# MLA layer: attention probabilities transposed by VectorE blocks and DMA instead of TensorE, with other DMA queues

## The chip, the cores and the metric

One core of one Trainium2 chip runs the whole program. The metric is the device time of one execution in microseconds (us); less is better.

## What is computed

The reference takes 512 tokens of width 1024 in fp32 through two layers and a last norm: an SSD (state space) layer, then a multi-head latent attention (MLA) layer with 16 heads. The change lies in the second layer:

```python
proj = u @ in_w
c_q, c_kv, k_r, z = proj[..., :o1], proj[..., o1:o2], proj[..., o2:o3], proj[..., o3:]
q = (rms_norm(c_q, q_norm_w) @ uq_w).reshape(bsz, seq, MLA_N_HEADS, MLA_QK_DIM)
kv = (rms_norm(c_kv, kv_norm_w) @ ukv_w).reshape(bsz, seq, MLA_N_HEADS, MLA_NOPE_DIM + MLA_V_DIM)
q_nope, q_rope = q[..., :MLA_NOPE_DIM], rope(q[..., MLA_NOPE_DIM:], positions)
o = causal_block_attention(q_full, k_full, v, MLA_QK_DIM ** -0.5)   # softmax in blocks of 128 queries
o = o.reshape(bsz, seq, MLA_WIDTH) * jax.nn.silu(z)
return o @ out_w
```

with 384 and 256 wide latents, head parts of 128 (plain) and 64 (rope), and values of 128.

## The kernel before

**Precision.** Every fp32 operand of a matmul is split into a high part in fp32r and the rest. ScalarE (ACT) casts the high part, VectorE (DVE) subtracts it to get the low part, and TensorE (PE) makes three passes: high by high, low by high, high by low. For weights this is `split_weight` (L266): a tile `raw` comes from HBM, ACT writes `whi` (L272), DVE writes `wlo` (L273). The pools hold 2 `raw`, 3 `whi` and 3 `wlo`; weights are loaded and split one ahead of their use (`LOOK`, `prefetch`). So the `whi` of a weight takes the buffer of the weight three before it, and can be written only when that one's gemm is done.

**Order.** PE's order is written by hand: it is the order in which the program issues its matmuls. DVE, ACT and the DMA queue of SyncE (SP) are ordered by a scheduler when the program is built; on the chip each engine takes its instructions strictly in that order. In the second layer everything that is in PSUM outside a few special tiles goes through `bank`, eight buffers of 128x512.

**A head.** The main loop (L884 and on) takes one head `h` at a time. Its gemms, the `feed`, belong to later heads: an even head runs `front_a` of the next pair of heads (the rope part `rraw`, the query `qh`/`ql`, the key `k`, with the weight `ua`) and a gemm for the gate `z`; an odd head runs `front_b` (query, key with the weight `ub`, and both halves of the values `va`/`vb` with the weight `uc`) and a gemm for `z`. Heads 11 to 15 have pieces of the output projection in place of gemms that have run out. Between the gemms `sched` (L237) places attention work: each piece stands at a fraction of the head's cost, from the tables at the top: `SC` for the four score blocks of the *next* head, `TU` for the four `turn` calls and `PR` for the four `product` calls of this head.

- `score(h, b)` makes scores of 128 queries by n keys on PE, a masked max on DVE (L805), the exp with its sum on ACT (L223), a reciprocal (L807) and a scale (L808) on DVE. The result `p` has queries in partitions.
- `turn(h, kb)` has PE transpose the blocks of key block `kb` (L817, ten 128x128 transposes a head) into a bank `pt`; ACT casts `ph` from it (L821), DVE subtracts `pl` (L822). `ph` and `pl` have two buffers each.
- `product(h, kb)` adds three matmuls to the head's bank `po` (L835): `ph` by `va`, `ph` by `vb`, `pl` by `va`. After the fourth, DVE multiplies `po` by `z` (L837).
- `rope` (L692) copies `rraw` with halves exchanged into `rsw`, by four DMAs, and makes two products and a sum on DVE (L697 to L699). `front_a` calls it once a pair of heads.

**Early in the layer** the first layer's output, transposed in 32x32 blocks by DVE into `ht` (L681), is stored by 32 small DMAs to `hd` in DRAM (L684): each writes 32 partitions of 16 blocks, which undoes the block order.

All of these DMAs, the weights included, go through SP's queue.

Of the kernel before, what the change touches and what calls it, by code (L numbers as in the profile page):

```python
# [10 lines left out]
F32 = mybir.dt.float32  # L11
F32R = mybir.dt.float32r
AF = mybir.ActivationFunctionType
ALU = mybir.AluOpType

P = 128
T = 512
D = 1024
KD = D // P
NCH = T // P  # L20
# [3 lines left out]
MH = 16  # L24
QL, KVL = 384, 256
# [14 lines left out]
P1 = (1.0, 2.4, 3.8, 12.0, 18.2)  # L40
GN = 16.84
G7 = 33.0
SF = (0.02, 0.1, 2.1, 3.1)
SC = (0.0, 0.16, 0.25, 0.44)
TU = (0.02, 0.08, 0.38, 0.55)
PR = (0.3, 0.48, 0.65, 0.94)
KO = (3, 4, 5, 8, 10)
MID = 4
NU = 1
# [2 lines left out]
SQ = 2  # L52
# [99 lines left out]
class Net:  # L152
# [8 lines left out]
    def build(self):  # L161
        tc, nc, ctx = self.tc, self.nc, self.ctx
        pool = lambda name, bufs, **k: ctx.enter_context(tc.tile_pool(name=name, bufs=bufs, **k))
        self.const = pool("const", 1)
        self.wraw = pool("wraw", 2)
        self.whi = pool("whi", 3)
        self.wlo = pool("wlo", 3)
        self.act = pool("act", 8)
        self.o16 = pool("o16", 16)
        self.nrm = pool("nrm", 1)  # L170
        self.res = pool("res", 8)
        self.dram = pool("dram", 1, space=bass.MemoryType.DRAM)

        const = self.const
        self.xs = []
        self.cols = const.tile([P, C_N], F32, name="cols")
        self.ident = const.tile([P, P], F32, name="ident")[:]
        self.rows = const.tile([P, 2 * NH], F32, name="rows")

        self.phase, self.group, self.before, self.head = "", [], [], None  # L180
        self.wq = []
        self.wpos = self.wload = 0
        self.wraws = []
        self.wready = {}
        for g in range(NG):
            for i in range(6):
                self.wq.append(("w", U_IN + 6 * g + i))
        for i in range(16):
            self.wq.append(("w", U_OUT0 + i))
        for i in range(6):  # L190
            self.wq.append(("w", U_M1 + i))
        self.wq += [("w", U_MZ + i) for i in range(3)] + [("ua", 0), ("w", U_MZ + 3), ("ub", 0), ("uc", 0), ("w", U_MZ + 4)]
        out = [("w", U_OUT1 + i) for i in range(16)]
        for h in range(14):
            j = h // 2 + 1
            self.wq += [("ua", j)] if h % 2 == 0 else [("ub", j), ("uc", j)]
            if h < 11:
                self.wq.append(("w", U_MZ + 5 + h))
            self.wq += [out.pop(0) for _ in range({11: 1, 12: 1, 13: 2}.get(h, 0))]
        self.wq += out  # L200

        with tc.tile_pool(name="ps_s", bufs=1, space=bass.MemoryType.PSUM) as ps, \
                tc.tile_pool(name="ssm", bufs=2) as wk:
            self.ps, self.wk = ps, wk
            self.ssm()
        with tc.tile_pool(name="ps_m", bufs=1, space=bass.MemoryType.PSUM, reuse_waits="tile") as ps, \
                tc.tile_pool(name="mla", bufs=2, reuse_waits="tile") as wk:
            self.ps, self.wk = ps, wk
            self.mla()

    LOOK = 1

# [47 lines left out]
    def load_weight(self, kind, idx):  # L260
        n = {"w": 1024, "ua": 1024, "ub": 640, "uc": 512}[kind]
        raw = self.wraw.tile([P, n], F32, tag="raw", name=self.nm("raw"))
        self.nc.sync.dma_start(raw[:], self.t[kind][idx])
        return raw

    def split_weight(self, raw, cuts=()):  # L266
# [383 lines left out]
    def mla(self):  # L650
        tc, nc, t, wk = self.tc, self.nc, self.t, self.wk
        v = nc.vector
        self.bufs = {"b": 8}
        col = lambda i: self.cols[:, i:i + 1]
        con = wk.tile([P, K_N - K_MASK], F32, name="con2", bufs=1)
        nc.sync.dma_start(con[:], t["con"][:, K_MASK:])
# [14 lines left out]
        for i in range(6):  # L671
            w = self.weight("w", U_M1 + i)
            ps = self.bank("mm")
            self.run(self.gemm(ps[:], w, vh, vl, KD))
            if i == NU:
                pss = self.sumsq([h[:] for h in self.h], D, "b")
                r1 = self.rstd_of(pss, D)
            if i >= 2:
                for k in (2 * i - 4, 2 * i - 3):
                    ht = wk.tile([P, T], F32, tag=("ph", "pl")[k % 2], name=self.nm("ht"))  # L680
                    v.transpose(ht[:], self.h[k][:])  # L681
                    for b in range(4):
                        m = slice(32 * b, 32 * b + 32)
                        nc.sync.dma_start(turned[:, :, k * P + 32 * b:k * P + 32 * b + 32],  # L684
                                          ht[m, :].rearrange("a (j b) -> a j b", b=32))
            pend.append(ps)
            while pend and i >= NU:
                o = self.o16.tile([P, T], F32, tag="o", name=self.nm("cq"))
                v.tensor_tensor(o[:], pend.pop(0)[:], r1[:], op=ALU.mult)
                cq.append(o)  # L690

        def rope(raw):  # L692
            sw = wk.tile([P, T], F32, tag="rsw", name=self.nm("rsw"), bufs=1)
            for i in range(4):
                j = i ^ 1
                nc.sync.dma_start(sw[32 * i:32 * i + 32, :], raw[32 * j:32 * j + 32, :])
            v.tensor_tensor(raw[:], raw[:], self.cosT, op=ALU.mult)  # L697
            v.tensor_tensor(sw[:], sw[:], self.sinT, op=ALU.mult)
            v.tensor_tensor(raw[:], raw[:], sw[:], op=ALU.add)  # L699
            return raw  # L700
# [77 lines left out]
                f["v"].append((va, vb))  # L778
                yield 1.3

        probs = [[] for _ in range(MH)]

        def score(h, b):
            f, i = F[h // 2], h % 2
# [21 lines left out]
            self.E(p[:], p[:], AF.Exp, scale=-1.0, bias=st[:, 0:1], accum_out=st[:, 1:2])  # L806
            v.reciprocal(st[:, 2:3], st[:, 1:2])  # L807
            v.tensor_scalar(p[:], p[:], st[:, 2:3], None, op0=ALU.mult)  # L808
            probs[h].append(p)

        parts, acc = [[] for _ in range(MH)], {}

        def turn(h, kb):
            n = T - kb * P
            pt = self.bank("pt")
            for b in range(kb, NCH):
                nc.tensor.transpose(pt[:, (b - kb) * P:(b - kb + 1) * P], probs[h][b][:, kb * P:(kb + 1) * P],  # L817
                                    self.ident)
            ph = wk.tile([P, T], F32R, tag="ph", name=self.nm("ph"))
            pl = wk.tile([P, T], F32R, tag="pl", name=self.nm("pl"))  # L820
            nc.scalar.copy(ph[:, :n], pt[:, :n])  # L821
            v.tensor_tensor(pl[:, :n], pt[:, :n], ph[:, :n].bitcast(F32), op=ALU.subtract)  # L822
            parts[h].append((ph, pl))

        def product(h, kb):
# [13 lines left out]
        def chain(*gs):  # L839
            for g in gs:  # L840
                yield from g
# [4 lines left out]
            yield from self.out_tok(zt, 0, hd)  # L846

        def norm(tiles, n, cw):
            at = (wk, ("qh", "ql", "s2") if n == KVL else ("ph", "pl", "s2"))
            pss = self.sumsq([x[:] for x in tiles], n, "b", *at)  # L850
            r = self.rstd_of(pss, n, *at)
            hs, ls = [], []
            for i, x in enumerate(tiles):
                v.scalar_tensor_tensor(x[:], x[:], col(cw + i), r[:], op0=ALU.mult, op1=ALU.mult)
                a = wk.tile([P, T], F32R, tag="ch", name=self.nm("ch"), bufs=5)
                b = wk.tile([P, T], F32R, tag="cl", name=self.nm("cl"), bufs=5)
                nc.scalar.copy(a[:], x[:])
                v.tensor_tensor(b[:], x[:], a[:].bitcast(F32), op=ALU.subtract)
                hs.append(a)
                ls.append(b)  # L860
            return hs, ls

        outg = out0()
        self.run(zgemm(0))
# [15 lines left out]
        self.run(zgemm(3))  # L880
        zsilu(0)
        self.run(fa)
        self.run(front_b(0))
        self.sched(zgemm(4), [(x, functools.partial(score, 0, b)) for b, x in enumerate(SF)])  # L884
        for h in range(MH):
            if h and h % 4 == 0:
                zsilu(h // 4)
            feed, cost = [], 0.0
            j = h // 2 + 1
            if h < 14:  # L890
                feed.append(front_a(j) if h % 2 == 0 else front_b(j))
                cost += 5.2 if h % 2 == 0 else 5.9
            if h < 11:
                feed.append(zgemm(5 + h))
                cost += 5.2
            if h >= 11:
                k = KO[h - 11]
                feed.append(itertools.islice(outg, k))
                cost += 1.3 * k
            at = SC if h + 1 < MH else ()  # L900
            pieces = [(x * cost, functools.partial(score, h + 1, b)) for b, x in enumerate(at)]
            pieces += [(x * cost, functools.partial(turn, h, b)) for b, x in enumerate(TU)]
            pieces += [(x * cost, functools.partial(product, h, b)) for b, x in enumerate(PR)]
            self.sched(chain(*feed), pieces)
# [166 lines left out]
```

## Time and profile before

| what | value |
|---|---|
| median of 3 runs | 837.02 us (836.73 to 837.34) |
| the profiled execution | 836.13 us |
| its span in the trace | 834.0 us |
| mean granted PE clock | 0.999 |
| PE busy | 819.3 us (98%) |
| DVE busy | 644.9 us (77%) |
| ACT busy | 450.4 us (54%) |
| GpSimd (POOL) busy | 0.2 us |
| DMA, share of 16 engines, queue of SP | 34.0% |

The profiled execution is one of many, and 2.1 us of its time lie outside the span. "Busy" of PE counts matmuls whose ends are modelled, so consecutive matmuls overlap in the records: a row's duration is longer than its place, which is the distance between two starts. Times in the timeline count from the start of the span. A group's row gives count, busy us and mean ns of one, and then the idle time of its engine just before it with what ended it. A name such as `ph<-pt` is output from input, by the program's tile names.

### The profile page before, as it was taken

How to read it: one execution, taken by the hardware profiler on the slowest of the kernel's cores; microseconds unless marked ns; L12 is line 12 of the kernel's file. 1: busy time of each engine (PE TensorE's matmuls, PEld its weight loads, DVE VectorE, ACT ScalarE, POOL GpSimd, SP SyncE). 2: the span in 40 equal slices, each digit the busy share in tenths (PEclk: the TensorE clock that was granted, in tenths of full speed). 3: DMA queues.
4: the chain of work that ended last, by engine and by line, in shares of the span. 5: the costliest groups of instructions: out<-in, count | busy, mean ns of one | idle time of the engine just before them, and what ended most of it. 6: DMA issues, size and time to landing. Idle time of an engine off the chain costs nothing.

```text
span 834.0 us, 11549 instructions
## 1 busy us (share of the span) xinstructions
PE 819.3 (98%) x4228; PEld 691.8 (83%) x4228; DVE 644.9 (77%) x1234; ACT 450.4 (54%) x794; POOL 0.2 (0%) x4
## 2 busy tenths in 40 slices
PE   7999999999999999999999999999999999999996
PEld 5887888888888888888888888888888888888885
DVE  7999898979787989778566787786767869675544
ACT  7567755545465657434353654556547557554233
POOL 0000000000000000000000000000000000000000
PEclk9999999999999999999999999999999999999999
DMA  6364543423242423333555142222222224331212
GB/s 227 103 191 141 155 147 106 152 99 129 101 139 90 152 76 127 115 121 94 130 130 132 54 130 64 79 72 76 63 64 58 90 78 152 101 97 56 86 66 101
DMA packets 50856, 90.55 MB, mean 109 GB/s; under 512 B 21552, under 2 KB 23088, under 8 KB 50800
## 3 DMA queue, kind: packets, MB, share of 16 engines
q1 hardware_dynamic: 50080, 88.77, 34.0%
q10 hardware_dynamic: 720, 1.05, 0.3%
q8 instruction: 33, 0.54, 0.3%
q14 instruction: 23, 0.19, 0.1%
HBM read 83.12 MB, written 4.33 MB: 105 GB/s over the span
## 4 chain that ended last, share of the span: by engine, by line
PE 92%; DVE 3%; DMA 2%; ACT 1%; SPq 1%; issue 0%; DVEq 0%; ACTq 0%
PE mm L291 55%; PE ot L941 11%; PE s L793 5%; PE mm L300 4%; PE po L835 4%; PE mm L773 3%; PE pt L817 2%; PE yd L138 2%; PE yd L291 1%; PE aux L130 1%; PE aux L105 1%; DMA x<-in_x_dram 1%; PE aux L77 1%; PE aux L89 1%; DMA L<-ac_d 1%; DVE wlo L273 1%
## 5 line engine op out<-in xcount | busy, mean ns | idle before, releaser
L272 ACT CAST whi<-raw 128x1024 fp32r<-128x1024 f32 (+3 forms) x132 | 127.0, 965 | 210.3 <-PE mm L291 172.8
L273 DVE TENSOR_TENSOR wlo<-raw,whi 128x1024 fp32r<-128x1024 f32 (+3 forms) x132 | 146.8, 1115 | 54.6 <-ACT whi L272 54.3
L291 PE MATMUL mm<-ah,whi 128*128 128x512 f32 x384 | 154.0, 401 | 0.0
L291 PE MATMUL mm<-ah,wlo 128*128 128x512 f32 x384 | 150.3, 391 | 0.4 <-DVE wlo L273 0.4
L291 PE MATMUL mm<-al,whi 128*128 128x512 f32 x384 | 149.9, 390 | 0.0
L291 PE MATMUL mm<-vh,whi 128*128 128x512 f32 x224 | 89.4, 399 | 0.8 <-ACT whi L272 0.8
L291 PE MATMUL mm<-vh,wlo 128*128 128x512 f32 x224 | 87.9, 392 | 0.7 <-DVE wlo L273 0.7
L291 PE MATMUL mm<-vl,whi 128*128 128x512 f32 x224 | 87.6, 391 | 0.0
L291 PEld LDWEIGHTS mm<-ah,wlo 128*128 128x128 f32 x384 | 72.1, 188 | 16.1 <-DVE wlo L273 0.8
L291 PEld LDWEIGHTS mm<-ah,whi 128*128 128x128 f32 x384 | 72.2, 188 | 15.3 <-issue 1.4
L291 PEld LDWEIGHTS mm<-al,whi 128*128 128x128 f32 x384 | 72.2, 188 | 14.4 <-DVE al L312 0.3
L941 PE MATMUL ot<-whi,ah 128*128 128x512 f32 (+1 forms) x136 | 52.4, 385 | 0.0
L941 PE MATMUL ot<-whi,al 128*128 128x512 f32 (+1 forms) x136 | 51.5, 379 | 0.0
L941 PE MATMUL ot<-wlo,ah 128*128 128x512 f32 (+1 forms) x136 | 51.4, 378 | 0.0
L291 PEld LDWEIGHTS mm<-vh,wlo 128*128 128x128 f32 x224 | 42.1, 188 | 10.7 <-DVE wlo L273 1.5
L291 PEld LDWEIGHTS mm<-vh,whi 128*128 128x128 f32 x224 | 42.2, 188 | 9.4 <-ACT whi L272 1.1
L223 ACT ACTIVATE p<-p,st 128x128 f32<-128x128 f32 (+1 forms) x64 | 36.1, 564 | 25.3 <-DVE st L805 25.2
L291 PEld LDWEIGHTS mm<-vl,whi 128*128 128x128 f32 x224 | 42.2, 188 | 7.3
L821 ACT CAST ph<-pt 128x512 fp32r<-128x512 f32 (+1 forms) x64 | 26.4, 421 | 33.3 <-PE pt L817 32.8
L291 PE MATMUL mm<-ch,whi 128*128 128x512 f32 x104 | 42.6, 410 | 0.0
L291 PE MATMUL mm<-ch,wlo 128*128 128x512 f32 x104 | 40.9, 393 | 0.0
L291 PE MATMUL mm<-cl,whi 128*128 128x512 f32 x104 | 40.8, 392 | 0.0
(223 smaller groups left out, 1637.7 us busy)
## 6 DMA issues: line engine op xcount, KB each, us to landing
raw<-in_w_dram SPq DMA_DIRECT2D x100, 512.0 KB, 3.3
L<-ac_d SPq DMA_DIRECT2D x32, 256.0 KB, 3.9
E<-ea_d SPq DMA_DIRECT2D x32, 128.0 KB, 3.5
raw<-in_ua_dram SPq DMA_DIRECT2D x8, 512.0 KB, 3.3
raw<-in_ub_dram SPq DMA_DIRECT2D x8, 320.0 KB, 2.8
x<-in_x_dram SPq DMA_DIRECT2D x8, 256.0 KB, 4.4
res<-in_x_dram SPq DMA_DIRECT2D x8, 256.0 KB, 3.1
hd<-ht SPq DMA_DIRECT2D x32, 64.0 KB, 3.5
```

What stands on the lines that cost most here:

```text
L138: nc.tensor.matmul(yd[64 * h:64 * h + 64, s], self.xdt[j][:, c, h, :], self.L[2 * j + h][:, s], start=True, stop=True)
L223: i = self.nc.scalar.activation(out, in_, func, **k)
L272: nc.scalar.copy(hi[:, a:b], raw[:, a:b])
L273: nc.vector.tensor_tensor(lo[:, a:b], raw[:, a:b], hi[:, a:b].bitcast(F32), op=ALU.subtract)
L291: self.nc.tensor.matmul(ps, a, b, start=i == 0, stop=i == len(seq) - 1)
L300: self.nc.tensor.matmul(p, seq[i][0], seq[i][1], start=i == 0, stop=i == 3 * ks - 1)
L773: nc.tensor.matmul(ps[:, c2 * 256:(c2 + 1) * 256], a, b, start=i == 0, stop=i == 5)
L793: nc.tensor.matmul(ps[:, :n], x[:, s], y[:, :n], start=k == 0, stop=k == 4)
L817: nc.tensor.transpose(pt[:, (b - kb) * P:(b - kb + 1) * P], probs[h][b][:, kb * P:(kb + 1) * P], self.ident)
L821: nc.scalar.copy(ph[:, :n], pt[:, :n])
L835: nc.tensor.matmul(po[:, kb * P:], x, y, start=kb == 0 and k == 0, stop=kb == NCH - 1 and k == 2)
L941: nc.tensor.matmul(ps[:, a:b], x, y, start=start and i == 0, stop=stop and i == 5)
```

## The change

- `score` ends with a transpose of `p` in 32x32 blocks on DVE into `pb` (L813 of the changed kernel) and four DMAs of SP that store it to a DRAM tile `pd` of the head's parity, in the block order that completes the transpose (L817).
- A new piece `fetch(h)` loads the four key blocks back into `pl` by four DMAs of SP (L833). It is the fifth entry of `SF` and `SC`.
- `turn` no longer uses PE: ACT casts `ph` from `pl` (L840) and DVE subtracts in place (L841). `pl` has a buffer for each key block, in two sets by the head's parity; the odd set uses tiles that the norms have left.
- In this layer SP's queue stands in the program's order instead of the scheduler's. Weights (`wqueue`) and the four rope DMAs are issued by GpSimd.
- The tables `SF`, `SC` and `PR` have other numbers, head 0's scores are placed across `front_b(0)` and `zgemm(4)`, `ht` takes only the two `ph` buffers, and a norm takes the tiles of `qh`/`ql`.

```diff
...
 GN = 16.84
 G7 = 33.0
-SF = (0.02, 0.1, 2.1, 3.1)
-SC = (0.0, 0.16, 0.25, 0.44)
+SF = (0.6, 1.0, 2.0, 3.2, 8.0)
+SC = (0.0, 0.1, 0.18, 0.28, 0.5)
 TU = (0.02, 0.08, 0.38, 0.55)
-PR = (0.3, 0.48, 0.65, 0.94)
+PR = (0.4, 0.56, 0.72, 0.94)
...
         self.phase, self.group, self.before, self.head = "", [], [], None
+        self.wqueue = nc.sync
...
                 tc.tile_pool(name="mla", bufs=2, reuse_waits="tile") as wk:
             self.ps, self.wk = ps, wk
-            self.mla()
+            with tc.manual_schedule(engines={mybir.EngineType.SP}):
+                self.mla()
...
         n = {"w": 1024, "ua": 1024, "ub": 640, "uc": 512}[kind]
         raw = self.wraw.tile([P, n], F32, tag="raw", name=self.nm("raw"))
-        self.nc.sync.dma_start(raw[:], self.t[kind][idx])
+        self.wqueue.dma_start(raw[:], self.t[kind][idx])
...
         v = nc.vector
         self.bufs = {"b": 8}
+        self.wqueue = nc.gpsimd
...
             if i >= 2:
                 for k in (2 * i - 4, 2 * i - 3):
-                    ht = wk.tile([P, T], F32, tag=("ph", "pl")[k % 2], name=self.nm("ht"))
+                    ht = wk.tile([P, T], F32, tag="ph", name=self.nm("ht"))
...
             for i in range(4):
                 j = i ^ 1
-                nc.sync.dma_start(sw[32 * i:32 * i + 32, :], raw[32 * j:32 * j + 32, :])
+                nc.gpsimd.dma_start(sw[32 * i:32 * i + 32, :], raw[32 * j:32 * j + 32, :])
...
                 yield 1.3
-        probs = [[] for _ in range(MH)]
+        pd = [self.dram.tile([T, T], F32, name=f"pd{i}") for i in range(2)]
...
             v.reciprocal(st[:, 2:3], st[:, 1:2])
             v.tensor_scalar(p[:], p[:], st[:, 2:3], None, op0=ALU.mult)
-            probs[h].append(p)
+            pb = wk.tile([P, T], F32, tag="pb", name=self.nm("pb"))
+            v.transpose(pb[:, :n], p[:])
+            turned = pd[h % 2][:].rearrange("(j a) q -> a j q", a=32)
+            for i in range(4):
+                q = b * P + 32 * i
+                nc.sync.dma_start(turned[:, :n // 32, q:q + 32],
+                                  pb[32 * i:32 * i + 32, :n].rearrange("a (j q) -> a j q", q=32))
         parts, acc = [[] for _ in range(MH)], {}
+
+        back = {}
+
+        def fetch(h):
+            for kb in range(NCH):
+                n = T - kb * P
+                if h % 2:
+                    g = ("sqa", "r0", "rt", "sq")[kb]
+                    pl = self.nrm.tile([P, T], F32R, tag=g, name=self.nm("pl"), bufs=SQ if g == "sq" else 1)
+                else:
+                    pl = wk.tile([P, n], F32R, tag=f"pl{kb}", name=self.nm("pl"), bufs=1)
+                pl = pl[:, :n]
+                nc.sync.dma_start(pl.bitcast(F32), pd[h % 2][kb * P:(kb + 1) * P, kb * P:])
+                back[h, kb] = pl
         def turn(h, kb):
             n = T - kb * P
-            pt = self.bank("pt")
-            for b in range(kb, NCH):
-                nc.tensor.transpose(pt[:, (b - kb) * P:(b - kb + 1) * P], probs[h][b][:, kb * P:(kb + 1) * P],
-                                    self.ident)
+            pl = back[h, kb]
             ph = wk.tile([P, T], F32R, tag="ph", name=self.nm("ph"))
-            pl = wk.tile([P, T], F32R, tag="pl", name=self.nm("pl"))
-            nc.scalar.copy(ph[:, :n], pt[:, :n])
-            v.tensor_tensor(pl[:, :n], pt[:, :n], ph[:, :n].bitcast(F32), op=ALU.subtract)
+            nc.scalar.copy(ph[:, :n], pl.bitcast(F32))
+            v.tensor_tensor(pl, pl.bitcast(F32), ph[:, :n].bitcast(F32), op=ALU.subtract)
...
         def norm(tiles, n, cw):
-            at = (wk, ("qh", "ql", "s2") if n == KVL else ("ph", "pl", "s2"))
+            at = (wk, ("qh", "ql", "s2"))
...
                 ls.append(b)
             return hs, ls
+
+        def steps(h):
+            return [functools.partial(score, h, b) for b in range(NCH)] + [functools.partial(fetch, h)]
...
         zsilu(0)
         self.run(fa)
-        self.run(front_b(0))
-        self.sched(zgemm(4), [(x, functools.partial(score, 0, b)) for b, x in enumerate(SF)])
+        self.sched(chain(front_b(0), zgemm(4)), list(zip(SF, steps(0))))
...
                 cost += 1.3 * k
             at = SC if h + 1 < MH else ()
-            pieces = [(x * cost, functools.partial(score, h + 1, b)) for b, x in enumerate(at)]
+            pieces = [(x * cost, fn) for x, fn in zip(at, steps(h + 1))]
```

Where instructions stand in the built programs, with buffer numbers. Lines of the changed kernel are two higher early in the file (L272 is L274, L223 is L225) and more later on. First ACT, in even head 6 of before, around the weight `uc` (`whi` 128x512). The cast of the head's first key block, `ph` 128x512, is the second row; the product that reads it stands on PE right behind the gemm of `k`.

```order
L272 CAST whi_5834<-raw_5713 128x640
L821 CAST ph_5742<-pt_5737 128x512
L223 ACTIVATE p_5730,st_5731<-p_5730,st_5731 128x128
L821 CAST ph_5750<-pt_5746 128x384
L731 COPY rraw_5757<-mm_5719 128x512
L223 ACTIVATE p_5786,st_5787<-p_5786,st_5787 128x256
L223 ACTIVATE p_5798,st_5799<-p_5798,st_5799 128x384
L311 CAST qh_5807<-mm_5773 128x512
L272 CAST whi_5895<-raw_5832 128x512
L721 CAST k_5818<-mm_5811 128x512
L821 CAST ph_5828<-pt_5825 128x256
```

ACT in the same head of the changed kernel, from the same `whi` 128x640; `ph` reads `pl` there.

```order
L274 CAST whi_5975<-raw_5833 128x640
L225 ACTIVATE p_5850,st_5851<-p_5850,st_5851 128x128
L225 ACTIVATE p_5875,st_5876<-p_5875,st_5876 128x256
L734 COPY rraw_5890<-mm_5839 128x512
L225 ACTIVATE p_5919,st_5920<-p_5919,st_5920 128x384
L313 CAST qh_5934<-mm_5906 128x512
L274 CAST whi_6029<-raw_5973 128x512
L225 ACTIVATE p_5944,st_5945<-p_5944,st_5945 128x512
L724 CAST k_5963<-mm_5956 128x512
L840 CAST ph_5863<-pl_5792 128x512
L840 CAST ph_5866<-pl_5794 128x384
```

The `ph` 128x512 has moved from second place to behind `whi` 128x512, the exp of the 128x512 scores and the cast of `k`. PE's product still stands right behind the gemm of `k` there.

Second, DVE in the same place of the changed kernel, from the low part of the query on; `pl` 128x512, which the third matmul of the product reads, is the last row. In before it stood ahead of all of these, behind the max (L805) of the next head's first score block.

```order
L314 TENSOR_TENSOR ql_5935<-mm_5906,qh_5934 128x512
L808 ISA p_5944,st_5945<-s_5938,con_3837 128x512
L808 ISA st_5945 128x1
L813 STREAM_TRANSPOSE pb_5881<-p_5875 128x256
L275 TENSOR_TENSOR wlo_6030<-raw_5973,whi_6029 128x512
L700 TENSOR_TENSOR rraw_5890<-rraw_5890,con_3837 128x512
L701 TENSOR_TENSOR rsw_5892<-rsw_5892,con_3837 128x512
L810 RECIPROCAL st_5945<-st_5945 128x1
L725 TENSOR_TENSOR k_5963<-mm_5956,k_5963 128x512
L702 TENSOR_TENSOR rraw_5890<-rraw_5890,rsw_5892 128x512
L841 TENSOR_TENSOR pl_5792<-pl_5792,ph_5863 128x512
```

Between `ql` and `wlo` before there was nothing, and behind `wlo` the same two rope products, `k` and the sum; the max of the fourth score block (L808), the block transpose of the second one (L813), the reciprocal and `pl` are new at this place.

Third, ACT in odd head 5, around the second half of the values; in before this was the order, with `ph` 128x512 in the second row:

```order
L272 CAST whi_5603<-raw_5519 128x1024
L821 CAST ph_5548<-pt_5543 128x512
L223 ACTIVATE p_5536,st_5537<-p_5536,st_5537 128x128
L821 CAST ph_5556<-pt_5552 128x384
L311 CAST qh_5563<-mm_5525 128x512
L272 CAST whi_5669<-raw_5601 128x1024
L721 CAST k_5574<-mm_5567 128x512
L223 ACTIVATE p_5583,st_5584<-p_5583,st_5584 128x256
L776 CAST va_5620<-mm_5607 128x512
L223 ACTIVATE p_5595,st_5596<-p_5595,st_5596 128x384
L272 CAST whi_5715<-raw_5667 128x1024
```

and in the changed kernel:

```order
L274 CAST whi_5781<-raw_5714 128x1024
L724 CAST k_5693<-mm_5686 128x512
L779 CAST va_5733<-mm_5720 128x512
L225 ACTIVATE p_5702,st_5703<-p_5702,st_5703 128x384
L274 CAST whi_5835<-raw_5779 128x1024
L840 CAST ph_5655<-pl_5584 128x512
L840 CAST ph_5658<-pl_5586 128x384
L225 ACTIVATE p_5743,st_5744<-p_5743,st_5744 128x512
L840 CAST ph_5772<-pl_5588 128x256
```

The first `ph` has moved behind the `whi` 128x1024 of the next head's gate weight (whose buffer the second half of the values frees). PE's first product, which stood between the two halves of the values, stands behind the second half now.

## Prediction

> **What bounds the kernel now.** I read the engine shares and the chain first. Columns: busy us, share of the span, instructions; then the shares of the chain that ended last.
>
> ```profile
> PE 819.3 (98%) x4228; PEld 691.8 (83%) x4228; DVE 644.9 (77%) x1234; ACT 450.4 (54%) x794; POOL 0.2 (0%) x4
> PE 92%; DVE 3%; DMA 2%; ACT 1%; SPq 1%; issue 0%; DVEq 0%; ACTq 0%
> ```
>
> TensorE (PE) bounds it. The windows view cuts that by stage: 60 to 350 us is the SSD layer, 495 to 770 the heads of the attention layer (busy us per engine, then clock and DMA share).
>
> ```profile
> 60.00:350.00 290.00, 289.00 (x1549) 241.75 (x1548) 253.56 (x446) 169.75 (x272) 0.00 (x0) 1.00 0.39 126
> 495.00:770.00 275.00, 275.00 (x1498) 238.98 (x1497) 203.14 (x493) 151.31 (x321) 0.00 (x0) 1.00 0.26 82
> ```
>
> In the heads PE is busy 275.00 of 275 us. So PE work taken out is gained in full, and every new wait of PE is lost in full. VectorE (DVE) has 72 us to spare, ScalarE (ACT) 124: what counts there is not how much they do but in which order, since each runs its queue in order.
>
> **What is removed.** The timeline of PE in head 5 (start, duration) shows nine of a head's ten transposes, seven in one place and two in another:
>
> ```profile
> 590.77 0.93 PE L817 MATMUL pt<-ident,p 128*128 128x128 f32 x7
> 591.45 0.48 PE L291 MATMUL mm<-ch,whi 128*128 128x512 f32 x1
> ...
> 598.65 0.38 PE L817 MATMUL pt<-ident,p 128*128 128x128 f32 x2
> 598.79 0.71 PE L793 MATMUL s<-k,qh 128*128 128x512 f32 x2
> ```
>
> Matmuls overlap, so I count start to start: seven cost 0.68, two 0.14, and the tenth at the pair's rate 0.07: 0.89 us a head, 14.2 over 16 heads. That is the whole gain to be had.
>
> **What is added on DVE.** Sixty-four block transposes. The grouped view (count | busy, mean ns | idle) has subtracts of falling width and a reduce; the tile view of `ht` (count, shortest/median/longest ns, first and last start) has the same transpose at full width, first:
>
> ```profile
> L681 DVE STREAM_TRANSPOSE ht<-res x8: 699/711/712, 388.2 to 431.6; 128x512 f32<-128x512 f32 x8
> ```
> ```profile
> L822 DVE TENSOR_TENSOR pl<-pt,ph 128x512 fp32r<-128x512 f32 x16 | 11.0, 689 | 3.7 <-ACT ph L821 3.7
> L805 DVE CUSTOM_DVE_ANT_0 p<-s,con 128x512 f32<-128x512 f32 x16 | 10.9, 682 | 0.2 <-PE s L793 0.2
> ...
> L822 DVE TENSOR_TENSOR pl<-pt,ph 128x256 fp32r<-128x256 f32 x15 | 6.3, 418 | 0.0
> ```
>
> Scaled as the subtracts (0.27 over two steps of width, 0.135 each), four widths cost 0.71+0.57+0.43+0.30 = 2.0 us a head, 32 in all: 235 us of DVE in a stage of 261 or more, 90% at most. The subtract and the cast, now from SBUF, are taken at their old prices. As a total DVE does not bind; its order does.
>
> **What is moved: the first cast and subtract.** Before, `ph` and `pl` of a head's first key block were made at its start (the order of ACT above has that cast ahead of two of the next head's exps). Now, in an even head, the cast stands behind `whi` of `uc`, the 128x512 exp and the cast of `k`. PE's first product still follows the `k` gemm directly. Here that point of head 6 as it ran: PE, ACT and DVE.
>
> ```profile
> 614.74 0.39 PE L291 MATMUL mm<-ch,wlo 128*128 128x512 f32 x1
> 614.97 0.39 PE L835 MATMUL po<-ph,va 128*128 128x512 f32 x1
> ...
> 615.43 0.40 PE L835 MATMUL po<-pl,va 128*128 128x512 f32 x1
> ```
> ```profile
> 614.94 0.62 ACT L272 CAST whi<-raw 128x512 fp32r<-128x512 f32 x1
> 615.47 0.58 ACT L721 CAST k<-mm 128x512 fp32r<-128x512 f32 x1
> 616.14 0.37 ACT L821 CAST ph<-pt 128x256 fp32r<-128x256 f32 x1
> ```
> ```profile
> 614.43 0.16 DVE L807 RECIPROCAL st<-st 128x1 f32<-128x1 f32 x1 [0.31 <-ACT p L223]
> ...
> 614.97 0.68 DVE L312 TENSOR_TENSOR ql<-mm,qh 128x512 fp32r<-128x512 f32 x1
> 615.60 0.69 DVE L273 TENSOR_TENSOR wlo<-raw,whi 128x512 fp32r<-128x512 f32 x1
> ...
> 616.81 0.69 DVE L698 TENSOR_TENSOR rsw<-rsw,con 128x512 f32<-128x512 f32 x1
> ...
> 618.61 0.42 DVE L822 TENSOR_TENSOR pl<-pt,ph 128x256 fp32r<-128x256 f32 x1
> ```
>
> `whi` cannot start sooner: its buffer is freed by the last matmul of the `k` gemm (614.94 beside 614.74). From the groups of ACT, the operations that now stand between:
>
> ```profile
> L223 ACT ACTIVATE p<-p,st 128x512 f32<-128x512 f32 x16 | 11.6, 724 | 5.3 <-DVE st L805 5.1
> L821 ACT CAST ph<-pt 128x512 fp32r<-128x512 f32 x16 | 9.4, 587 | 26.0 <-PE pt L817 26.0
> ```
>
> ACT: 614.94 + 0.53 (`whi`, start to start) + 0.72 (exp) + 0.67 (`k`) + 0.59 (`ph`) = 617.45. The first product matmul waits 2.5 us. DVE: from `wlo` at 615.60 five operations at 0.60 each to 618.61, the reciprocal 0.16, then `pl` 0.69: 619.46. The third matmul, due at 615.43, comes 4.0 late. Ahead of `wlo` now stand a reduce (0.68) and a 256-wide transpose (0.43); if `ql` moves up little, 1.1 more. So 4.0 to 5.1 in all; I take 4.2, since `qh` loses the `ph` casts before it. Seven even heads (0 to 12) have this: 29.4 us.
>
> In an odd head `po` follows the second `v` gemm, which ended at 598.65, and the cast stands behind a 128x1024 `whi` whose buffer that gemm frees. ACT and DVE of head 5 there:
>
> ```profile
> 598.85 1.05 ACT L272 CAST whi<-raw 128x1024 fp32r<-128x1024 f32 x1 [0.94 <-PE mm L773]
> 599.80 0.37 ACT L821 CAST ph<-pt 128x256 fp32r<-128x256 f32 x1
> ```
> ```profile
> 599.94 1.23 DVE L273 TENSOR_TENSOR wlo<-raw,whi 128x1024 fp32r<-128x1024 f32 x1 [1.37 <-ACT whi L272]
> 601.08 0.42 DVE L822 TENSOR_TENSOR pl<-pt,ph 128x256 fp32r<-128x256 f32 x1
> ```
>
> `ph` is ready at 599.80 + 0.59 = 600.39 (wait 1.7), `pl` at 601.08 + 0.69 = 601.77 where the third matmul was due at 599.11: 2.7 us, seven odd heads, 18.6. Heads 14 and 15 and the three places where silu stands in ACT's queue I put at 2 (0 to 10). The other edits I cost at nothing: head 0's scores move ahead of `zgemm(4)`, the same PE work beside the same gemms, and the norm's other buffers are used when no query needs them. `ht` has two buffers now: the third transpose waits for four issues and a landing of the first, 2.0 + 3.5 = 5.5 us, the fourth 2.0 more; two gemms' weights lie ready meanwhile. If that cover fails it is 2 us for each of three pairs, inside the 10.
>
> **The DMAs.** SP issues 16 small writes and 4 reads a head, POOL the weights and rope.
>
> ```profile
> raw<-in_w_dram SPq DMA_DIRECT2D x100, 512.0 KB, 3.3
> hd<-ht SPq DMA_DIRECT2D x32, 64.0 KB, 3.5
> ```
> ```profile
> 606.74 0.69 DVE L711 TENSOR_TENSOR z<-mm,rr 128x512 f32<-128x512 f32 x1 [2.47 <-PE mm L291]
> ```
> ```profile
> L684 SPq DMA_DIRECT2D hd<-ht x32: 341/487/856, 389.0 to 448.9; - x32
> ```
>
> `hd<-ht` is the same kind of write. After the 512-wide transpose: four issues of 0.49, 3.5 to land, one issue, 3.5 back, 9.4 us in all. In an odd head eight operations of DVE, from the second `pl` to that transpose, follow the first `pl`: 0.55 + 0.16 + 0.42 + 0.69 + 0.57 + 0.29 + 0.69 + 0.71 = 4.1, an estimate from the widths above with the scale at a subtract's 0.69, so it ends near 601.77 + 4.1 = 605.9. The head's last gemm ended at 606.7 (DVE's first wait of head 6, above) and now ends 2.7 later, 3.5 after the transpose. The first `pl` is then there 9.4 − 3.5 = 5.9 us into the next head; the cast wants it at 616.86, which is 10.1 after 606.7. Nothing, with 4.2 of slack. SP runs in the program's order, and a write that waits for its transpose holds up only the reads behind it, which need it anyway: the weights and rope have left that queue.
>
> Weights: their 3.3 us run while `whi` waits for a buffer of PE's (the 0.94 above); nothing. Rope: `rsw` starts from `rraw`.
>
> ```profile
> L696 SPq DMA_DIRECT2D rsw<-rraw x32: 512/586/602, 479.1 to 716.1; - x32
> DMA to landing us min/median/max: 1.9/2.0/2.2
> ```
> ```profile
> 610.51 0.60 ACT L731 COPY rraw<-mm 128x512 f32<-128x512 f32 x1
> ```
>
> The sum: 611.1 + 4 × 0.59 + 2.0 = 615.5, wanted at 616.81. POOL's price per issue is in no row; between SP's own price and twice it (617.9, 1.1 late). I take it as SP's.
> The Trainium skill ("SBUF — State Buffer", the box on VectorE blocking DMA) speaks against this: descriptors of GpSimd's queue are written by GpSimd, which is locked out while VectorE runs an operation that takes both ports. No run here shows it; it bears on the third rival.
>
> **Sum.** 836.13 − 14.2 + 29.4 + 18.6 + 2 = 871.9. The median of the runs lies 0.9 above the profiled one: **873**. With only the ACT part of the waits (7 × (2.5 + 1.7) = 29.4) it is 852; with 5.1 in even heads and 10 for the rest 887.
>
> **Rivals.**
> First, faster: PE does not wait. That PE's transposes go is sure from the code, so 14.2 is gained whatever else happens. It needs ACT and DVE to reach the cast before the gemm ends, or a wait below 0.89 us a head (the break-even). Then 837.0 − 14.2 = 823. For it: 124 us of spare ACT. Against: `whi`, which stands ahead of the cast, itself needs the gemm's end. 0.07; another 0.03 that partial waits cancel the gain (837).
>
> Second, the PE clock drops in the waits. The cold start and the end of the run:
>
> ```profile
> 4.79 0.80 PE L300 MATMUL mm<-vh,whi 128*128 128x512 f32 x1 [4.79 <-ACT whi L272]
> ...
> 9.29 0.39 PE L300 MATMUL mm<-vl,whi 128*128 128x512 f32 x1
> ```
> ```profile
> 826.70:828.70 2.00, 0.03 (x1) 0.00 (x0) 1.89 (x9) 1.42 (x5) 0.00 (x0) 1.00 0.39 143
> ...
> 830.70:831.80 1.10, 0.00 (x0) 0.00 (x0) 0.00 (x0) 0.00 (x0) 0.00 (x0) 1.00 1.03 384
> ```
>
> Cold, ten matmuls took 4.50 us instead of 2.3: 2.2 per drop, 15 in the even heads, 31 in all: 888 to 904. Against it: at the end the clock stays 1.00 for 5.1 us without a matmul, and my waits are 2.5 and 1.6.
> The Trainium skill ("TensorE: Matmul & The Clock Gate", Part 1) halves the clock after one idle window of about 3.4 us; by it the 2.5 us keep it, the 4.2 together need not. The trace's end agrees with a limit above 3.4. 0.10.
>
> Third, rope through POOL comes 2 us late: the sine product, and with it `pl`, moves by 2 in seven heads, 887. 0.08. From the 1.3 us of slack shown it starts to cost.
>
> My forecast has the rest, 0.72, within 852 to 887. Slower by over 0.2% is 0.90 in all, within 0.2% (1.7 us, about what a measurement can tell) 0.03, faster 0.07. The range 850 to 900 leaves out the faster cases and most of a full clock drop.
>
> **What would show it.** Right: PE idle before L854 in each head, named after ACT `ph` and DVE `pl`, some 4 us in even and 2.7 in odd heads; no L817 transposes on PE; clock 1.00. Wrong: no idle before L854, or `pl<-pd` DMA or `rsw` as releaser, or `raw` late.

## The result, and the profile after

| | before | changed |
|---|---|---|
| median | 836.94 us (4 runs) | 913.31 us (908.79 to 915.52, 4 runs) |
| profiled execution, span | 836.13, 834.0 us | 908.79, 906.5 us |
| PE busy | 819.3 us | 838.2 us |

The ratio is 1.091 (95% interval 1.088 to 1.094): slower, as forecast, but by 76 us where 36 were forecast, outside the range of 850 to 900. First the engine shares of the changed kernel, the heads' window, and PE's list of waits (us in all, times, longest):

```profile
PE 838.2 (92%) x4068; PEld 694.7 (77%) x4068; DVE 673.7 (74%) x1298; ACT 451.2 (50%) x794; POOL 50.8 (6%) x100
```
```profile
495.00:770.00 275.00, 236.44 (x1101) 196.47 (x1100) 190.57 (x458) 128.47 (x268) 29.77 (x58) 0.90 0.48 118
```
```profile
PE po L854 <- ACT ph L840: 38.2, 16, 4.4
PE po L854 <- DVE pl L841: 13.0, 12, 1.7
```

Three things are to be seen. PE, busy 275 of 275 us in that window before, is busy 236 of 275. And its granted clock, 1.00 before, is 0.90: PE has 160 instructions fewer and is still busy 19 us longer. The waits stand where they were forecast, before the products, on the cast and on the subtract, 51.2 us in all. In head 6 PE's timeline reads:

```profile
640.64 0.39 PE L293 MATMUL mm<-ch,wlo 128*128 128x512 f32 x1
643.22 0.50 PE L854 MATMUL po<-ph,va 128*128 128x512 f32 x1 [2.19 <-ACT ph L840]
643.55 0.40 PE L854 MATMUL po<-ph,vb 128*128 128x512 f32 x1
645.30 0.80 PE L854 MATMUL po<-pl,va 128*128 128x512 f32 x1 [1.35 <-DVE pl L841]
645.90 0.63 PE L293 MATMUL mm<-vh,whi 128*128 128x512 f32 x1
646.33 0.63 PE L293 MATMUL mm<-vl,whi 128*128 128x512 f32 x1
```

Matmuls of this width start 0.23 us apart when nothing holds them, so the first product matmul was due at 640.87 (640.64 + 0.23); it came 2.35 us late. The third was due at 641.33 and came 3.97 late. Behind it the gemm's matmuls take 0.63 and stand 0.43 apart, near the 0.45 of the cold start (ten in 4.50 us). The odd head 5 has the same in small:

```profile
620.48 0.28 PE L776 MATMUL mm<-whi,cl 128*128 128x256 f32 x1
622.41 0.50 PE L854 MATMUL po<-ph,va 128*128 128x512 f32 x1 [1.65 <-ACT ph L840]
...
623.75 0.80 PE L854 MATMUL po<-pl,va 128*128 128x512 f32 x1 [0.61 <-DVE pl L841]
```

The third matmul, due at 621.06, came 2.7 late. The clock, in windows of 3.41 us laid on the moments at which it changed (PE busy us comes first, the granted clock is the third number from the end):

```profile
620.34:623.75 3.41, 1.15 (x6) 0.51 (x5) 2.51 (x6) 2.69 (x5) 0.36 (x1) 1.00 0.38 94
623.75:627.17 3.42, 3.42 (x8) 2.74 (x9) 1.77 (x5) 0.41 (x1) 0.18 (x1) 0.50 0.44 104
627.17:630.58 3.41, 3.41 (x18) 2.91 (x18) 1.60 (x3) 0.79 (x2) 0.00 (x0) 1.00 0.20 36
535.01:538.42 3.41, 1.76 (x12) 1.17 (x10) 2.51 (x7) 2.40 (x6) 0.00 (x0) 1.00 0.47 124
```

A window in which PE was busy a third of the time (1.15 of 3.41) is followed by one at half clock with 8 matmuls, and that, PE having been busy throughout, by one at full clock with 18. The last row is a window half busy (1.76 of 3.41): nothing dropped behind it. Over the heads 21 such windows run at half clock, 71.7 us in all. PE is busy for 61.8 us of that time, and at full clock the same work would take half as long, so it costs 30.9 us.

The balance from PE's first to its last matmul in the two profiled executions, 821.9 us before and 894.2 after: transposes −18.4 (e4_no_turn below), idle time of PE +53.2 (2.7 to 55.9), half clock +30.9, and +6.5 that is left. For this rest there is only an estimate: the first matmul behind a wait holds PE for 0.33 to the next start instead of 0.23 (643.22 and 643.55 above), and the last one ahead of the wait counts as busy for its whole 0.39 instead of its place of 0.23. For the 28 waits of the list that is 28 × 0.26 = 7.3.

### The profile page after: what moved, and what is told of

Its sections match the earlier page's. It is cut to its first block, busy times and chain, and to the rows that moved or that the text cites. A ratio compares the mean times of both kernels' runs of the same rounds, so it can differ in the third digit from the quotient of the medians.

```text
span 906.5 us, 11929 instructions
## 1 busy us (share of the span) xinstructions
PE 838.2 (92%) x4068; PEld 694.7 (77%) x4068; DVE 673.7 (74%) x1298; ACT 451.2 (50%) x794; POOL 50.8 (6%) x100
## 5 line engine op out<-in xcount | busy, mean ns | idle before, releaser
L274 ACT CAST whi<-raw 128x1024 fp32r<-128x1024 f32 (+3 forms) x132 | 126.9, 964 | 228.9 <-PE mm L293 189.4
L293 PE MATMUL mm<-vh,whi 128*128 128x512 f32 x224 | 94.6, 422 | 0.8 <-ACT whi L274 0.8
L293 PE MATMUL mm<-vh,wlo 128*128 128x512 f32 x224 | 93.9, 419 | 1.2 <-DVE wlo L275 1.2
L293 PE MATMUL mm<-vl,whi 128*128 128x512 f32 x224 | 93.7, 418 | 0.0
L225 ACT ACTIVATE p<-p,st 128x128 f32<-128x128 f32 (+1 forms) x64 | 35.9, 561 | 59.3 <-DVE st L808 59.3
L841 DVE TENSOR_TENSOR pl<-pl,ph 128x512 fp32r<-128x512 f32 (+1 forms) x64 | 30.0, 488 | 39.9 <-ACT ph L840 39.7
L854 PE MATMUL po<-ph,va 128*128 128x512 f32 (+1 forms) x64 | 23.1, 361 | 38.2 <-ACT ph L840 38.2
L265 POOL DMA_DIRECT2D raw<-in_w_dram x36 | 19.4, 539 | 670.0 <-DMA hd<-ht 417.6
L293 PEld LDWEIGHTS mm<-vh,wlo 128*128 128x128 f32 x224 | 45.7, 204 | 12.6 <-DVE wlo L275 2.1
L293 PEld LDWEIGHTS mm<-vh,whi 128*128 128x128 f32 x224 | 46.4, 207 | 10.1 <-ACT whi L274 1.0
L840 ACT CAST ph<-pl 128x512 fp32r<-128x512 f32 (+1 forms) x64 | 27.8, 456 | 51.9 <-PE po L854 46.0
L293 PEld LDWEIGHTS mm<-vl,whi 128*128 128x128 f32 x224 | 46.1, 206 | 9.5
```

Source lines behind the costliest of these rows:

```text
L225: i = self.nc.scalar.activation(out, in_, func, **k)
L265: self.wqueue.dma_start(raw[:], self.t[kind][idx])
L274: nc.scalar.copy(hi[:, a:b], raw[:, a:b])
L293: self.nc.tensor.matmul(ps, a, b, start=i == 0, stop=i == len(seq) - 1)
L840: nc.scalar.copy(ph[:, :n], pl.bitcast(F32))
L841: v.tensor_tensor(pl, pl.bitcast(F32), ph[:, :n].bitcast(F32), op=ALU.subtract)
```

## The experiments

Theory A: the 51 us come from the order on ACT and DVE, and most of the rest from the clock that these waits bring down. Its rivals are named in the expectations.

**e1_fill.** The idle time filled with spare matmuls:

```diff
+            if kb == 0 and h < 14:
+                for _ in range(8 if h % 2 == 0 else 6):
+                    nc.tensor.matmul(po[:], vh[0][:, :P], vh[0][:], start=True, stop=True)
             seq = [(va[:, s], ph[:, :n]), (vb[:, s], ph[:, :n]), (va[:, s], pl[:, :n])]
```

> The changed kernel with idle-time filler: PE gets 8 (even heads) or 6 (odd heads) spare 128x512 matmuls right ahead of the first product of heads 0 to 13, written to the product's own bank, which the product then overwrites; at 0.23 us each that is 1.8 and 1.4 us of PE work, less than the 2.5 and 1.7 us that PE waits there. Theory A (the 51 us of waits come from the order of ACT and DVE, and the other 36 us from the PE clock, halved after each window of 3.4 us in which PE was busy for less than about half): the waits stay, the filler hides in them, the granted clock goes from 0.96 to 1.00 and the time falls to about 875 (865 to 885). Rival B (the 36 us come from elsewhere: later weights or rope, more DMA traffic): the time stays at 909 to 915, or rises by the 22 us of filler work if the waits were not there to hide it.

Measured 915.62 us (ratio 1.093, 1.091 to 1.096). The time did not fall to the forecast 865 to 885, and this run alone decides nothing, since one wait of 16.4 us is new, in head 13. Its cause is SP's queue, in order. SP's timeline (a row can gather several issues), and the cast that waited:

```profile
754.05 1.76 SPq L833 DMA_DIRECT2D pl<-pd  x4
755.86 34.74 SPq L947 DMA_DIRECT2D hr<-hd  x8
790.65 9.26 SPq L817 DMA_DIRECT2D pd<-pb  x16
801.62 1.76 SPq L833 DMA_DIRECT2D pl<-pd  x4
```
```profile
804.19 1.06 ACT L840 CAST ph<-pl 128x512 fp32r<-128x512 f32 x2 [15.03 <-DMA pl<-pd]
```

The eight `hr` loads of the output projection wait for buffers (30.2 us of it until DVE's subtract `al`, by SP's list of waits); all probability writes of the next head stand behind them for 34.7 us.

**e5_fill_hr and e6_hr.** The same eight loads on ACT's queue, with the filler and without:

```diff
-                    nc.sync.dma_start(r[n][:], hd[c, :, n * T:(n + 1) * T])
+                    nc.scalar.dma_start(r[n][:], hd[c, :, n * T:(n + 1) * T])
```

> The kernel e1_fill with one thing more: the eight hr loads (first layer's output, read back for the output projection), which stand in SP's in-order queue ahead of the probability writes of the last heads, are issued by ACT. Theory A: in e1_fill these loads held SP's queue for some 20 us near 790 us and made the one 16.4 us wait of head 13; without that the filler shows what the clock cost: at most three or four drops of the clock in the heads, 49 us of waits less the 16 and about 2 us of filler each hidden in them, total 870 to 888. Rival B (the 36 us beside the waits are not the clock): 905 or more.

> The changed kernel with only the eight hr loads moved from SP's queue to ACT's. Theory A: in the changed kernel itself they hold the queue only a little; the waits of heads 11 and 13 (4.4 and 3.9 us) fall by 0 to 3 us in all, so the time is 905 to 915. Rival F (SP's in-order queue is a large part of the loss): below 895.

Measured 892.32 us with the filler (1.067, 1.064 to 1.070) and 904.24 without (1.080, 1.078 to 1.083). The second lies just below its expected 905 to 915 and far above rival F's 895, which falls. So the loads cost the changed kernel 6 to 9 us (9.1 between the medians 913.3 and 904.2, 5.7 between the two profiled executions): PE's waits in heads 11 and 13 fell from 4.4 and 3.9 to 3.5 and 2.5, and the time at half clock in the heads from 71.7 to 61.4. And a kernel with 98 extra matmuls, 22 us of PE work, is 12 us faster than the one without. The window from 515 to 734 us, which holds heads 0 to 10 of the kernel without filler, first without and then with it:

```profile
515.00:734.00 219.00, 186.09 (x859) 153.40 (x859) 150.11 (x358) 97.52 (x206) 24.07 (x46) 0.90 0.48 119
```
```profile
515.00:734.00 219.00, 199.48 (x985) 164.79 (x983) 161.42 (x377) 104.13 (x217) 24.62 (x47) 0.98 0.50 123
```

In the same 219 us the filled kernel got through 126 matmuls more at 0.98 of the clock. Its waits are shorter by what the filler covered (first without, then with):

```profile
PE po L854 <- ACT ph L840: 35.2, 16, 3.5
PE po L854 <- DVE pl L841: 13.4, 13, 1.9
```
```profile
PE po L857 <- DVE pl L841: 15.5, 13, 2.1
PE po L857 <- ACT ph L840: 15.0, 15, 3.4
```

18 us of waiting went (48.6 to 30.5) for 22 us of filler, so by that alone the kernel would be 4 us slower; it is 12 faster, and the 16 us between are the clock: PE was busy for 55.1 us at half clock without the filler and 18.7 with it, half of which is 18. Rival B falls. The expected 870 to 888 was missed by 4: parts of the waits were not covered, three drops of the clock stayed in heads with filler, and two came in heads 14 and 15, which have none.

**e2_order.** Order alone. An edge that only orders two instructions of one engine, without a wait, puts the first `ph` and `pl` ahead of what they stood behind:

```diff
+            if kb == 0:
+                self.first, self.nsplit = (h, a, b), 0      # a: cast ph, b: subtract pl
...
+            if self.first and self.nsplit == 2 + self.first[0] % 2:   # whi and wlo
+                self.link(x, [self.first[1]])
+                self.link(y, [self.first[2]])
```
(the comments in this cut and in that of e9_order3 are added here) and likewise for the products of `rope`, the casts and subtracts of `k` (even heads), `va`, `vb`, and the max and exp of the last score blocks.

> The changed kernel with only the order of ACT and DVE altered: order-only edges put the first cast ph and the first subtract pl of each head ahead of the whi/wlo, exp, k and rope operations that they stood behind. The DMAs and their queues are those of the changed kernel. Theory A: the pl tiles have landed about 6 us into a head, the waits before the first product go from 51 us to under 8, the clock stays at 1.00, and the time is 836 less 14 for the PE transposes plus what is left: 823 to 832. Rival C (the round trip through DRAM or the GpSimd queue is late, order or not): the first cast then waits for the DMA pl<-pd, with everything now queued behind it, and the time stays above 860.

Measured 865.11 us (1.034, 1.032 to 1.035), 48 us faster than the changed kernel with every DMA where it was. So the order was the larger cause; but the forecast of 823 to 832 failed, and the time is the one that rival C gave, above 860. Waits of 28 us are left:

```profile
PE po L874 <- ACT ph L858: 12.7, 10, 5.0
PE po L874 <- DVE pl L859: 11.1, 8, 2.4
PE po L874 <- DVE st L823: 3.9, 1, 3.9
```
```profile
622.42 0.62 ACT L858 CAST ph<-pl 128x512 fp32r<-128x512 f32 x1 [1.72 <-DMA pl<-pd]
```

The cast now stands early and waits for the DMA: with the chain gone the round trip through DRAM is one of the next things, as rival C had it. It is not all of what is left: the waits on casts, most of which stand behind that DMA, are 12.7 us, and most of the 11.1 on subtracts is the order of DVE again (the place is shown under e8_best). The round trip alone does not hold the time above 860: e9_order3 below keeps it and takes 843.96.

**e3_queues.** The kernel before with only the queue part: weights and rope on GpSimd (`wqueue`), SP in the program's order.

> The kernel before with only the queue part of the change: weights and rope issued by GpSimd in the MLA layer, SP in the program's order; PE still transposes. Theory A: no difference, 835 to 839. Rival D (GpSimd's slower issue makes rope or weights late): each of seven even heads loses 1 to 2 us, 845 or more.

Measured 838.00 us (1.0011, 1.0003 to 1.0020): slower by about a microsecond, 1.7 at most. The issues of rope on POOL and their landing:

```profile
L699 POOL DMA_DIRECT2D rsw<-rraw x32: 496/499/513, 481.6 to 718.1; - x32
...
DMA to landing us min/median/max: 1.8/1.9/3.8
```

0.50 each to issue, 1.9 to land, no more than on SP. In the changed kernel itself the same DMAs took longer to land, 3.7 us (median), and that is what the prediction's third rival feared; but DVE sat idle for them only twice, 1.5 us in all. Rival D falls.

**e4_no_turn.** The kernel before without PE's transposes:

```diff
-            pt = self.bank("pt")
-            for b in range(kb, NCH):
-                nc.tensor.transpose(...)
+            pt = probs[h][NCH - 1]
```

> The kernel before with PE's 160 transposes left out: ph and pl are made from the untransposed probabilities of the last query block, so the attention output is another one; the work of ACT and DVE is the same. It prices the gain. Forecast: 14 us, so 821 to 825. Rival E (a bound just behind PE takes the gain back): 830 or more.

Measured 817.87 us (0.977, 0.976 to 0.979), 19 us faster, more than forecast. PE's busy time is the number to read:

```profile
PE 800.9 (98%) x4068; PEld 675.1 (83%) x4068; DVE 645.0 (79%) x1234; ACT 453.5 (56%) x794; POOL 0.2 (0%) x4
```

18.4 less than before. Start to start the transposes hold 13.6 of it; the matmul behind each group pays too. In the kernel before, after the seven transposes of head 5 (its first gemm matmul started at 591.45):

```profile
591.77 0.40 PE L291 MATMUL mm<-cl,whi 128*128 128x512 f32 x1
592.00 0.40 PE L291 MATMUL mm<-ch,wlo 128*128 128x512 f32 x1
```

0.32 to the second matmul instead of 0.23: 0.09 for each of 48 groups is 4.3 us, and 13.6 + 4.3 = 17.9.

**e7_late_hr.** e6_hr with `PR = (0.62, 0.75, 0.87, 0.99)`.

> e6_hr with the products later on PE: PR = (0.62, 0.75, 0.87, 0.99), so that 9 to 12 gemm matmuls (2.1 and 2.7 us) stand between the point where the casts are released and the first product. Order of the chain on ACT and DVE is unchanged. Theory A: waits in even heads fall from 3.6 to about 1.5 us, in odd heads from 2.3 to about 0; with so little idle time in any window of 3.4 us the clock stays at 1.00; 836 - 18 for the transposes + 18 left = 834 to 848. Rival G (the waits move along, because the third and fourth product now want their casts closer behind the first): 860 or more.

Measured 875.99 us (1.047, 1.045 to 1.049). The expected 834 to 848 was missed by far. Of the odd heads 1, 5 and 9 lost their waits, as expected, 3 and 7 kept 1.7 us, where silu stands ahead of the cast, and 11 and 13 kept 3.2 and 2.8. Most even heads kept theirs, against the expectation. ACT and PE in head 6 show why:

```profile
632.30 0.62 ACT L738 CAST s<-rraw 64x512 fp32r<-64x512 f32 x1 [2.04 <-DVE rraw L702]
632.94 0.61 ACT L739 CAST s<-rraw 64x512 fp32r<-64x512 f32 x1
633.58 1.03 ACT L840 CAST ph<-pl 128x512 fp32r<-128x512 f32 x2
```
```profile
634.25 0.50 PE L854 MATMUL po<-ph,va 128*128 128x512 f32 x1 [2.89 <-ACT ph L840]
```

The expectation took ACT's order for unchanged. The scheduler had moved the cast again, behind the rope casts (`s<-rraw`), which themselves wait for DVE. That is rival G, whose 860 or more came, by another road: PE's point moved, and the queue's with it.

**e8_best.** Both remedies together, e2_order's edges and e7_late_hr's table and loads.

> Both remedies at once: order-only edges of e2_order, the later products of e7_late_hr, hr loads on ACT. Theory A: the order edges take the chain off the gemm's end, the later products cover the DRAM round trip of about 9.5 us that e2_order waited for; waits under 10 us, clock 1.00, 820 to 830, which would be faster than the kernel before. Rival C (the round trip still binds): 840 or more.

Measured 859.32 us (1.028, 1.024 to 1.032); the forecast of 820 to 830 failed. DVE and PE in head 6:

```profile
631.22 0.68 DVE L752 TENSOR_TENSOR s<-rraw,s 64x512 fp32r<-64x512 f32 x1
631.94 0.69 DVE L753 TENSOR_TENSOR s<-rraw,s 64x512 fp32r<-64x512 f32 x1
632.66 0.48 DVE L829 TENSOR_SCALAR p<-p,st 128x512 f32<-128x512 f32 x1
633.06 0.42 DVE L859 TENSOR_TENSOR pl<-pl,ph 128x256 fp32r<-128x256 f32 x1
```
```profile
631.21 0.28 PE L874 MATMUL po<-ph,vb 128*128 128x256 f32 x1
633.53 0.39 PE L874 MATMUL po<-pl,va 128*128 128x256 f32 x1 [2.04 <-DVE pl L859]
```

The first product is free now and the third waits: its `pl`, the third key block, stands in DVE's queue behind the rope subtracts. The time is rival C's 840 or more, but not its mechanism, since the releaser is DVE and not the DMA.

**e9_order3.** e8_best with edges for that place too:

```diff
+            if kb == 2:
+                for i in self.after2:            # the rope sum, s1 and s2
+                    self.link(i, [b])
+                for i in self.after2[1:]:
+                    self.link(i, [self.st3])     # the 128x512 block transpose
```
and the same edge from that transpose to `wlo` of `uc` and to the gate's product with its gemm.

> e8_best with more order-only edges on DVE: in even heads the subtract pl of the third key block goes ahead of the rope sum and of the s1/s2 subtracts that held it 2.0 to 2.5 us behind PE's third product in e8_best, and the 512-wide block transpose goes ahead of the gate's product with the gemm. Theory A (the loss is where the casts and subtracts stand in the in-order queues, plus the clock drops that the waits cause): the nine waits of about 2.2 us (20 us) and the five clock drops in the heads (17 us at half clock, 8 us lost) go: 859 less 20 to 28, 828 to 840, about level with the kernel before or faster. Rival C (the DRAM round trip binds under everything): another wait, for the DMA pl<-pd, takes their place and the time stays at 850 or more.

Measured 843.96 us (1.008, 1.005 to 1.010). PE's waits on the products are down to 13 us, and the heads run at 0.99 of the clock:

```profile
PE po L886 <- ACT ph L864: 6.8, 4, 3.9
PE po L886 <- DVE pl L865: 5.4, 11, 1.2
PE po L886 <- DVE st L827: 1.2, 1, 1.2
```
```profile
495.00:770.00 275.00, 260.30 (x1317) 220.51 (x1316) 220.14 (x542) 148.47 (x314) 35.11 (x67) 0.99 0.60 150
```

The longest wait, 3.9 us in head 11, stands behind a cast that waits for the DMA, and the one drop of the clock follows it, so something of rival C is left, though not its 850 or more:

```profile
709.15 0.62 ACT L864 CAST ph<-pl 128x512 fp32r<-128x512 f32 x1 [4.67 <-DMA pl<-pd]
```

Of the 76 us the change cost, 69 are undone by the places of instructions alone (and the `hr` loads' queue), with the DRAM round trip, the transposes on DVE and the GpSimd queue kept. The expected 828 to 840 was missed by 4. It is not faster than the kernel before: PE's idle time is 19.1 us where it was 2.7, 13.4 of it before the products, and its busy time 810.6, 9.7 above e4_no_turn's, of which 3.0 is the drop of the clock; so the 18 us saved are given back.

## Why the prediction was wrong, point by point

1. *PE binds, so new waits are lost in full.* Right: e4_no_turn turns PE work removed into time, one for one.
2. *Transposes: 14.2 us.* Too small: 18.4. The step counted start to start within the groups and left out the matmul behind each.
3. *Even heads 4.2, odd heads 2.7, sum 48 and 2 for the rest.* Right in mechanism, and in size where it was worked out. In head 6 the working gave 2.5 and 4.0, measured 2.35 and 3.97; in head 5 1.7 and 2.7, measured 1.8 and 2.7. The allowance of 1.1 for the reduce and the transpose ahead of `wlo` was not needed. The total, 51.2 in the list of waits against 50, is nearer than its parts, and that is luck: the seven even heads hold 25.4 where 29.4 were forecast, the seven odd ones 20.8 where 18.6 were, with the most in heads 11 and 13 (the `hr` loads), and heads 14 and 15 hold 5.0 where 2 were put down for them and the places of silu. The list also counts idle time, which is shorter than lateness (2.19 beside 2.35 in head 6). e2_order shows the order as the main cause of these waits.
4. *DMA and queues cost nothing.* Right for weights and rope (e3_queues), though rope landed later than taken, and for the round trip as long as the order holds the casts back; there the slack of 4.2 us was real only beside the late cast, and without it the trip is one of the next things waited for. It was wrong in one place: "a write that waits for its transpose holds up only the reads behind it". It overlooked the `hr` loads, which wait for buffers in the same in-order queue, 6 to 9 us by e6_hr.
5. *The clock stays at 1.00.* This step failed, and it carries most of the miss. The profiled execution, 908.8, is 36.9 us above the sum of 871.9: 30.9 of that is the clock, 6.5 the rest of the balance, 3.2 more idle time than the 50 forecast, −4.2 the transposes, and 0.5 lies outside PE's work. The prediction put 0.10 on the rival "the PE clock drops in the waits" and gave 31 us for it; it happened, and cost 30.9. That the two agree so closely is partly luck: the price was 2.2 for one drop in each of 14 heads, taken from the cold start; there were 14 drops, but seven lasted one window and seven two. The reason given against it was that at the end of the run the clock stayed up for 5.1 us without a matmul while the waits would be 2.5 and 1.6. That reading took the time since the last matmul for what counts. The changes of the clock lie whole multiples of 3.413 us apart through the whole run, so what counts is the share of a fixed window: over the ten traces other than that of before all 70 drops (the one at each end included) followed a window in which PE was busy for 0.52 of it or less, and no window under 0.46 passed without one. The end of the run before fits. Its last two windows on the grid at full clock:

```profile
825.05:828.47 3.42, 1.68 (x14) 1.47 (x13) 2.94 (x12) 2.78 (x12) 0.00 (x0) 1.00 0.41 153
828.47:831.88 3.41, 0.00 (x0) 0.00 (x0) 1.08 (x4) 1.16 (x2) 0.00 (x0) 1.00 0.66 246
```

The window that the last matmul fell into was half busy (1.68 of 3.42) and passed; the drop came behind the empty one.
The Trainium skill ("TensorE: Matmul & The Clock Gate", Part 1) has the free-running window of about 3.4 us, and the trace agrees with its length and its grid; it asks for an idle window, and here windows that were a third busy were enough (1.15 of 3.41 us above). The measurement decides.

Forecast and rival two were not alternatives: the waits of the forecast are the condition of the rival. Had the price been multiplied with the question "is PE busy for half of each 3.4 us?", 4.0 us of lateness in an even head would have raised a doubt; the half itself could not be read from the trace before, where one half-busy window passed and only an empty one did not. What stays open is the rest of 6.5 us in the balance, which is estimated and not tested, and what would become of the last 13 us of waits in e9_order3, 5.3 of them behind casts that wait for the DMA; that was not tried.

## What to carry to other kernels

When a tile comes from DRAM instead of from PE, read in the new order what the engines that consume it have queued ahead of it: the place in an in-order queue decides, not the engine's spare time. On a kernel that keeps PE full, price each new wait twice: its own length, and a window at half clock whenever it leaves PE idle for about half of 3.4 us. And put nothing that waits for a buffer into a queue that carries a latency-bound round trip.

## What the runs showed of the hardware

- PE's clock is decided in windows of 3.413 us on a fixed grid; in these traces a window busy for less than about half (0.46 to 0.52) is followed by one at half clock. A half-clock window that is itself not nearly full is followed by another: all 60 that were followed by full clock were busy for 0.83 or more (one busy for 0.93 was followed by another too). In the changed kernel even heads mostly paid 6.83 us, odd heads 3.41.
- Idle PE costs more than useless PE: 98 spare matmuls made a kernel 12 us faster (904.2 to 892.3).
- The matmul behind a group of transposes holds PE 0.09 us longer (0.32 to the next start instead of 0.23), 4.3 us over the 48 groups.
- The 64 KB block writes `pd<-pb` landed in 1.9 us (median) where `hd<-ht`, the row that the prediction took for them, needed 3.5; the reads `pl<-pd` behind them took 2.7 at full width, but 4.5 for the narrowest.
